# A two-layer diffusion transformer block on one core: z transposed whole behind the scores, squares moved behind the scores, partial sums stored by SyncE's queue

## The chip, the cores and the metric

The kernel runs on one core of one Trainium2 chip. The metric is the device time of one execution in microseconds (us), the median of three runs. A core has five engines that run at the same time, each through its own queue of instructions: PE (TensorE, with its weight loads listed apart as PEld), DVE (VectorE), ACT (ScalarE), POOL (GpSimd) and SP (SyncE, which only starts transfers). A transfer is issued from the queue of SP or ACT, waits there for what it needs, and holds up what stands behind it in that queue.

## The reference

Two layers work on 1024 latent tokens and 256 context tokens of width 1024, all in f32:

```python
p = h @ w_in                        # h: modulated RMS norm of x; hc likewise of the context
a_in, b_in, q, k, v, g = ...        # column ranges of p
q, k = rope(rms_norm(q)), rope(rms_norm(k))
s = q @ k.T * QK_DIM ** -0.5        # 4 heads, 2 maps each, keys of context and latents
p = softmax(s); p = p[0] - lam * p[1]
o = rms_norm(p @ v) * (1 - lam_init)
y = concat(fourier_mix(a_in), pool_mix(b_in), o) * silu(g)
x = x + gate * (y @ w_out)
```

The context tokens are updated in the first layer only, and attend to the context alone. Shift, scale and gate come from a conditioning vector times `w_mod`, for each layer.

## The kernel before, in words

Each f32 operand of a large product is split into two parts, high and low, and a product is three matmuls. The order on each engine is the order in which the code is written; nothing is rescheduled. Tiles come from rotating pools: `T5` and `E2` in SBUF, `PX` for banks of PSUM. `full` is true in layer 0, which also treats the ten tiles of latents and context (numbers 0 to 7 and 8, 9).

A layer has two phases. In the first (called phase A below) it builds the modulated rows H, mixes the Fourier and pooling heads, and computes half of the output projection, the part that needs no attention: `for hf in range(2): for j in range(nA)`, 12 matmuls (L751), DVE's product with the gate (L755), POOL's addition of the residual (L757), and a store of the partial sum to `xpart` (L759). `r_load` (L723) loads the residual two steps ahead through SP. Behind each step `next(bg)` runs one step of a background generator; in layer 0 that is `mod1`, the modulation of layer 1, whose weights are loaded through ACT's queue (L198) and summed by DVE (L207, L209, `total` with L237). Then follow the K, Q and V projections. K and Q use rotary tables that POOL makes (L773) from `gq`, `rcos` and `rsin`, loaded by SP (L764 to L767); L798 is the last step of a K or Q tile on DVE, and L786 its transposes on PE.

The second phase is attention, a loop of units (tile j, head h), four to a tile; in layer 0 there are two context units among them, at 4 and 13. That gives 34 units in layer 0 and 32 in layer 1. Step i runs parts of several units: transposes of the probabilities of unit i-2 (`p_trans`, L966, copied by ACT L971 and DVE L969), the scores of unit i (L899), row maxima (L908), exponentials (L923), products with V of unit i-2 (L982), the normalization by head (L985, L993, L1009), and pieces of the output projection of finished tiles (`out_proj`, L1048, added in L1051). The scores of a unit lie in two tiles of three PSUM banks each (one per map, `SS[0]` and `SS[1]`); `spare(cur, m)` hands out the last 256 columns of one of them before the scores are written. `q_trans` transposes the queries of the next tile into a `PX` bank behind the scores; `z_trans` transposes a finished tile's gated output z, in two halves, in the spare columns of `SS[1]` ahead of the scores. Both split the transposed rows with `trans_split`: PE transposes (L876), two copies by ACT (L877, L878) and a subtraction by POOL (L879). The four pieces of 256 columns follow at steps set by `PIECES`, `CTXP` and `LAST`. Tile 7, the last, is done in the tail.

In layer 0 a finished tile's rows are also squared and summed (`x_rms`, two halves, L265, driven by `tile_rms`) at the end of a step, and scaled by the result (L1065) for layer 1. Layer 0's tail is interleaved with the first rows of layer 1 (`h_block`; L279, L285; L1213 scales tiles that were reloaded). `wa_split`'s pieces split the output weights in early units (ACT L316, POOL L317).

Of the kernel before, what the change touches and what calls it, by code (L numbers as in the profile page):

```python
# [18 lines left out]
D = 1024  # L19
# [12 lines left out]
def build(tc, I, out):  # L32
# [156 lines left out]

    def mod_acc(src, c0, sides, res, eng2=None):  # L190

        acc = T5([128, 2, 512])
        res.append(acc)
        ws = []

        def load(kp):
            w = T5([128, 2, 512])
            act.dma_start(w, src[2 * kp:2 * kp + 2, :, c0:c0 + 512].rearrange("k p c -> p k c"))  # L198
            ws.append(w)
        load(0)  # L200
        load(1)
        yield
        for k in range(KT):
            for s in sides:
                a, w, sk = acc[:, s, :], ws[k // 2][:, k % 2, :], sc[:, k, s:s + 1]
                if k == 0:
                    dve.tensor_scalar(a, w, sk, None, MULT)  # L207
                else:
                    dve.scalar_tensor_tensor(a, w, sk, a, MULT, ADD)  # L209
            if k % 2 and k // 2 + 2 < KT // 2:  # L210
                load(k // 2 + 2)
            yield
# [15 lines left out]
    def mod1():  # L228
# [11 lines left out]
        for q in range(4):  # L240
            accs = []
            for n, _ in enumerate(mod_acc(I["wmB"], q * 512, (0, 1), accs)):
                if n == 4 and last is not None:
                    total(q - 1, last)
                yield
# [285 lines left out]
    def layer(l, src, dst, carry):  # L531
# [208 lines left out]
        for hf in range(2):  # L740
# [3 lines left out]
            for j in range(nA):  # L744
# [13 lines left out]
                r_load(hf * nA + j + 2)  # L758
                act.dma_start(xpart[l][j][:, sl], x)  # L759
                next(bg, None)  # L760
# [85 lines left out]
        k_trans(0)  # L846
        k_trans(0)
        st = {}

# [20 lines left out]

        def trans_split(rows, to, ps, h0, n):

            sl = slice(h0 * 128, h0 * 128 + n * 128)
            for h in range(n):
                o = (h0 + h) * 128
                pe.transpose(ps[:, h * 128:h * 128 + 128], rows[:, o:o + 128], ident)  # L876
            act.activation(to[0][:, sl], ps[:, :n * 128], AF.Copy)  # L877
            act.activation(rows[:, sl], ps[:, :n * 128], AF.Copy)  # L878
            pool.tensor_tensor(to[1][:, sl], rows[:, sl], to[0][:, sl].bitcast(F32), SUB)  # L879

        def q_trans(j):
            st[j]["Q"] = parts(j)
            trans_split(st[j]["q"], st[j]["Q"], PX(), 0, NH)

# [66 lines left out]

        def spare(cur, m):

            return st[cur]["SS"][m][:, 1280:1536] if cur else PX()

        def p_trans(u, t0, cur=None):
# [6 lines left out]
            n = min(4, nkt - t0)  # L963
            ps = spare(cur, 0) if t0 == 8 else PX()
            for i in range(n):
# [44 lines left out]

        def z_trans(j, half, cur):
            s = st[j]
            if half == 0:
                s["z"] = parts(j)
            trans_split(s["g"], s["z"], spare(cur, 1), 2 * half, 2)

# [13 lines left out]

        PIECES = [(c, 256, 2 + c // 256) for c in range(0, D, 256)]
        CTXP = [(c, 256, 3 + c // 256) for c in range(0, D, 256)]
        LAST = {7: [(0, 512, 2), (512, 512, 3)]} if full else {7: [(0, 512, 2), (512, 256, 3), (768, 256, 3)]}
        LAST.update({8: CTXP, 9: CTXP})
        ENDS = () if full else (6, 7)
# [38 lines left out]
        for i, u in enumerate(units):  # L1076
            first.setdefault(u[0], i)
        q_load(0)
        vv = []
# [15 lines left out]
        def step(i):  # L1095
# [3 lines left out]
            done = units[i - 3] if 0 <= i - 3 < N else None  # L1099

            fin = {d: units[i - 2 - d][0] for d in range(7)
                   if 0 <= i - 2 - d < N and units[i - 2 - d][1] in (NH - 1, -1)}
            if old and old[1] in (2, -1):
                out_load(old[0])
            if cur:
                st[cur] = dict(S=[], p=[], l=[], SS=[PS(), PS()])
            if old:
                p_trans(old, 0)
                p_trans(old, 8, cur)
            for d, half in ((1, 0), (2, 1)):  # L1110
                j = fin.get(d)
                if j is not None and j < 7:
                    z_trans(j, half, cur)
            for d, half in ((2, 0), (3, 1)):
                if fin.get(d, 0) >= 8:
                    z_trans(fin[d], half, cur)
            if old:
# [27 lines left out]
            yield  # L1145
            for d, j in sorted(fin.items(), key=lambda f: f[1]):
                for c0, m, at in LAST.get(j, PIECES):
                    if d == at:
                        out_proj(j, c0, m)
            if fin.get(1) == 7:  # L1150
                z_last(7)
            while rms:
                if next(rms[0], rms) is rms:
                    rms.pop(0)
                elif cur:
                    break
            if full:
                for d, j in fin.items():
                    if d == LAST.get(j, PIECES)[-1][2]:
                        rms.append(tile_rms(j))  # L1160
            yield
# [175 lines left out]
```

## Time and profile before

| | before |
|---|---|
| median of three runs | 1462.04 us (1458.29 to 1462.25) |
| the profiled execution | 1462.49 us, span 1460.7 us |
| granted TensorE clock, mean | 0.978 |
| PE, PEld busy | 1371.1 us (94%), 1223.1 us (84%) |
| DVE, ACT, POOL busy | 857.6 us (59%), 534.3 us (37%), 779.7 us (53%) |
| layer 0's attention, first and last scores start at | 522.1, 778.7 us |
| layer 1's attention, first and last scores start at | 1167.8, 1430.3 us |

The span is what the profiler shows of the execution's own time; 1.8 us lie around it. Busy shares are over the whole span. In the rows below, a timeline row gives start, duration, engine, line, operation, output and inputs, and in brackets the idle time before it and what ended it; a group's row gives count, busy time, mean of one in ns, and idle time before the group with what ended it. An engine name with q (ACTq, SPq) is its queue of transfers; a transfer's row there shows how long its issue held the queue, waits for its inputs included.

### The profile page before, as it was taken

The numbers are of one execution on the slowest core, as the hardware profiler recorded it, in microseconds if no ns is written. First come the engines' busy times: TensorE is split into PE (matmuls) and PEld (weight loads), VectorE is DVE, ScalarE is ACT, GpSimd is POOL, SyncE is SP. The second block draws the span as 40 slices with busy tenths as digits, with TensorE's granted clock in tenths as the row PEclk, the third lists the DMA queues.
The fourth block names the chain that finished last, engine by engine and source line by source line (L and its number), as shares of the span: only waits on it lengthen the run. The fifth ranks groups of instructions, "written<-read, shape, count | busy, mean of one in ns | idle before, by whom it ended". The sixth has DMA issues, their size and how long they took to land.

```text
span 1460.7 us, 24849 instructions
## 1 busy us (share of the span) xinstructions
PE 1371.1 (94%) x9828; PEld 1223.1 (84%) x9828; DVE 857.6 (59%) x1338; ACT 534.3 (37%) x1178; POOL 779.7 (53%) x867
## 2 busy tenths in 40 slices
PE   7899999897999978999998899999999998999998
PEld 1688899787999967978887778887999986788887
DVE  2853467787873056767665654573455225777775
ACT  2633111101221256565554432211131225665663
POOL 2543122457583057777775743226757217777774
PEclk9999999998999999999999999999999999999999
DMA  9320242584232022120213221526402210121111
GB/s 361 111 69 33 100 137 95 194 270 138 73 106 83 1 94 87 50 76 22 87 38 116 98 65 37 204 79 204 154 30 95 73 44 25 34 70 62 44 38 58
DMA packets 65155, 137.11 MB, mean 94 GB/s; under 512 B 7312, under 2 KB 19728, under 8 KB 65040
## 3 DMA queue, kind: packets, MB, share of 16 engines
q1 hardware_dynamic: 49712, 108.82, 22.3%
q10 hardware_dynamic: 15328, 26.72, 5.3%
q8 instruction: 77, 1.26, 0.4%
q14 instruction: 38, 0.31, 0.1%
HBM read 105.63 MB, written 29.88 MB: 93 GB/s over the span
## 4 chain that ended last, share of the span: by engine, by line
PE 36%; ACT 6%; DVE 5%; POOL 2%; issue 2%; DVEq 0%; ACTq 0%; POOLq 0%
PE x L359 13%; PE S L899 6%; PE x L339 5%; ACT t L923 4%; PE x L982 3%; PE x L751 3%; PE x L1048 2%; DVE sm L908 2%; PE x L966 1%; POOL t L288 1%; PE S L876 1%; POOL t L1052 0%; DVE e L285 0%; ACT t L286 0%; PE x L876 0%
## 5 line engine op out<-in xcount | busy, mean ns | idle before, releaser
L359 PE MATMUL x<-wh,t 128*128 128x256 f32 x2432 | 449.6, 285 | 0.0
L359 PEld LDWEIGHTS x<-wh,t 128*128 128x128 f32 x2432 | 383.0, 192 | 1.8 <-issue 1.0
L359 PE MATMUL x<-wl,t 128*128 128x256 f32 x1216 | 344.8, 284 | 0.0
L908 DVE TENSOR_REDUCE sm<-S 128x1 f32<-128x1280 f32 (+1 forms) x132 | 189.6, 1478 | 191.3 <-PE S L899 191.3
L359 PEld LDWEIGHTS x<-wl,t 128*128 128x128 f32 x1216 | 234.0, 192 | 1.3 <-issue 1.2
L923 ACT ACTIVATE t<-S,sm 128x1280 f32<-128x1280 f32 (+1 forms) x140 | 172.6, 1238 | 151.2 <-DVE sm L908 137.8
L339 PE MATMUL x<-t,wh 128*128 128x512 f32 (+1 forms) x640 | 174.2, 382 | 9.2 <-DVE t L288 4.6
L899 PE MATMUL S<-t,e 64*128 64x512 f32 (+1 forms) x1152 | 149.3, 381 | 24.2 <-ACT t L971 20.7
L982 PE MATMUL x<-t,t 128*128 128x128 f32 x1312 | 164.8, 282 | 6.3 <-DVE t L969 6.3
L982 PEld LDWEIGHTS x<-t,t 128*128 128x128 f32 x1312 | 154.2, 194 | 13.0 <-DVE t L969 6.5
L899 PEld LDWEIGHTS S<-t,e 64*128 64x128 f32 x1152 | 111.4, 193 | 61.8 <-ACT t L971 29.9
L339 PEld LDWEIGHTS x<-t,wh 128*128 128x128 f32 x640 | 114.5, 192 | 32.8 <-POOL t L288 6.2
L317 POOL TENSOR_TENSOR wl<-st,wh 128x1024 fp32r<-128x1024 f32 x36 | 93.9, 2609 | 87.3 <-ACT wh L316 87.3
L946 POOL TENSOR_TENSOR t<-t,t 128x768 f32<-128x768 f32 (+1 forms) x64 | 115.0, 1796 | 5.3
L316 ACT ACTIVATE wh<-st 128x1024 fp32r<-128x1024 f32 x64 | 65.0, 1063 | 135.6 <-DMA xpart<-e 53.3
L1048 PE MATMUL x<-wh,e 128*128 128x256 f32 (+1 forms) x488 | 105.5, 299 | 0.8 <-ACT e L1024 0.7
L339 PE MATMUL x<-t,wl 128*128 128x512 f32 (+1 forms) x320 | 100.6, 375 | 3.4 <-DVE wl L317 3.4
L751 PE MATMUL x<-wh,t 128*128 128x512 f32 x288 | 93.9, 405 | 7.8 <-DVE t L527 4.7
L209 DVE SCALAR_TENSOR_TENSOR t<-t,sc,t 128x512 f32<-128x512 f32 x98 | 90.7, 968 | 3.8 <-DMA t<-in_wmB_dram 3.4
L1048 PEld LDWEIGHTS x<-wh,e 128*128 128x128 f32 x488 | 80.7, 191 | 2.9 <-ACT e L1024 1.3
L997 POOL TENSOR_SCALAR sm<-sm,sm 128x1 f32<-128x1 f32 x64 | 16.9, 264 | 122.6 <-ACT t L993 116.6
L966 PE MATMUL x<-ident,t 128*128 128x128 f32 x520 | 79.6, 276 | 1.7 <-ACT t L971 0.9
(233 smaller groups left out, 2287.6 us busy)
## 6 DMA issues: line engine op xcount, KB each, us to landing
st<-in_w_in_dram SPq DMA_DIRECT2D x48, 512.0 KB, 4.5
t<-in_wmB_dram ACTq DMA_DIRECT2D x24, 512.0 KB, 5.3
xpart<-e ACTq DMA_DIRECT2D x36, 256.0 KB, 4.8
t<-xpart SPq DMA_DIRECT2D x18, 512.0 KB, 4.8
t<-in_wmS_dram SPq DMA_DIRECT2D x16, 512.0 KB, 8.5
st<-in_w_out_dram SPq DMA_DIRECT2D x16, 512.0 KB, 3.9
t<-in_x_dram SPq DMA_DIRECT2D x10, 512.0 KB, 10.3
e<-in_x_dram SPq DMA_DIRECT2D x20, 256.0 KB, 5.1
```

The costliest lines, as they stand in the source:

```text
L209: dve.scalar_tensor_tensor(a, w, sk, a, MULT, ADD)
L317: lo_eng[hf].tensor_tensor(lo[:, sl, :], st, hi[:, sl, :].bitcast(F32), SUB)
L339: pe.matmul(p[:, :m], lhsT=W[wi][:, k, ct * 128:ct * 128 + 128], rhs=H[k][hi][:, c0:c0 + m], start=(n == 0), stop=(n == 3 * KT - 1))
L359: pe.matmul(bank[:, i * 256:i * 256 + 256], lhsT=H[k][hi][:, j * 128:j * 128 + 128], rhs=W[wi][:, k, :], start=(n == 0), stop=(n == 3 * KT ...
L751: pe.matmul(ps, lhsT=zr[k][zi][:, j * 128:j * 128 + 128], rhs=W[wi][:, k, :], start=(n == 0), stop=(n == 11))
L899: pe.matmul(S[m][:, i * nk + c:i * nk + c + w], lhsT=Q[q][r, h * 128:h * 128 + 128], rhs=k[h][r, k0 + c:k0 + c + w], start=(n == 0), stop= ...
L908: dve.tensor_reduce(nb, S[:, :nh * nk].rearrange("p (h k) -> p h k", h=nh), AX.X, ALU.min)
L923: act.activation(p[:, sl], S[:, sl], AF.Exp, bias=nb[:, i:i + 1], scale=-1.0, accum_out=ls[:, i:i + 1])
L946: pool.tensor_tensor(p[0][:, cut:end], p[0][:, cut:end], p[1][:, cut:end], ADD)
L966: pe.transpose(ps[:, i * 128:i * 128 + 128], s["p"][0][:, (t0 + i) * 128:(t0 + i + 1) * 128], ident)
L982: pe.matmul(o[:, i * 128:i * 128 + 128], lhsT=s["PT"][:, i * nkt + t, :], rhs=vv[h][:, kt0 + t, :], start=(t == 0), stop=(t == nkt - 1))
L1048: pe.matmul(ps[:, :m], lhsT=s["z"][zi][:, k * 128:k * 128 + 128], rhs=Wa[hf][wi][:, k, w0:w0 + m], start=(n == 0), stop=(n == 11))
```

## The change

1. `z_trans` transposes all four heads at once into a `PX` bank, behind the scores and `q_trans`, by the same `trans_split` that `q_trans` uses. A small plan (`at_z`, `at_out`, `at_x`, `at_end`) replaces the tables: z of a tile comes at first + 8 (first + 5 for a context tile) or at the next step that no `q_trans` or other z has taken, the pieces in the four steps behind it, the load of the partial sum one step ahead of it. Before, the halves came at first + 6 and first + 7 (of tiles 0 to 6) and the pieces at first + 7 to first + 10.
2. The squares of `tile_rms` are issued behind the scores and transposes instead of at the step's end.
3. The stores to `xpart` go through SP's queue instead of ACT's.
4. `mod_acc` waits `lead` background steps between its first two loads and their first use (two in `mod1`), issues the third and fourth load at the start of steps 2 and 4 instead of at the end of steps 1 and 3, and what is left of the background generator runs behind the Q projection.

```diff
--- before.py
+++ after.py
@@ mod_acc @@
-    def mod_acc(src, c0, sides, res, eng2=None):
+    def mod_acc(src, c0, sides, res, lead=1):
...
-        yield
+        for _ in range(lead):
+            yield
         for k in range(KT):
+            if k in (2, 4):
+                load(k // 2 + 1)
...
-            if k % 2 and k // 2 + 2 < KT // 2:
-                load(k // 2 + 2)
             yield
@@ mod1 @@
-            for n, _ in enumerate(mod_acc(I["wmB"], q * 512, (0, 1), accs)):
+            for n, _ in enumerate(mod_acc(I["wmB"], q * 512, (0, 1), accs, 2)):
@@ half output projection @@
                 r_load(hf * nA + j + 2)
-                act.dma_start(xpart[l][j][:, sl], x)
+                sp.dma_start(xpart[l][j][:, sl], x)
                 next(bg, None)
@@ behind Q @@
         k_trans(0)
+        for _ in bg:
+            pass
@@ attention @@
-        def trans_split(rows, to, ps, h0, n):
...
+        def trans_split(rows, to):
+
+            ps = PX()
+            for h in range(NH):
+                pe.transpose(ps[:, h * 128:h * 128 + 128], rows[:, h * 128:h * 128 + 128], ident)
+            act.activation(to[0], ps, AF.Copy)
+            act.activation(rows, ps, AF.Copy)
+            pool.tensor_tensor(to[1], rows, to[0].bitcast(F32), SUB)
...
-            ps = spare(cur, 0) if t0 == 8 else PX()
+
+            ps = st[cur]["SS"][0][:, 1280:1536] if cur and t0 == 8 else PX()
...
-        def z_trans(j, half, cur):
-            s = st[j]
-            if half == 0:
-                s["z"] = parts(j)
-            trans_split(s["g"], s["z"], spare(cur, 1), 2 * half, 2)
+        def z_trans(j):
+            st[j]["z"] = parts(j)
+            trans_split(st[j]["g"], st[j]["z"])
...
-        PIECES = [(c, 256, 2 + c // 256) for c in range(0, D, 256)]
-        CTXP = [(c, 256, 3 + c // 256) for c in range(0, D, 256)]
-        LAST = {7: [(0, 512, 2), (512, 512, 3)]} if full else {7: [(0, 512, 2), (512, 256, 3), (768, 256, 3)]}
...
+        taken = {f - 1 for f in first.values()}
+        for j in sorted(first, key=first.get):
+            e = first[j] + (1 if j >= 8 else NH)
+            if j == 7:
+                plan(at_z, e + 2, j)
+                sizes = (512, 512) if full else (512, 256, 256)
+                steps_of = (e + 3, e + 4, e + 4)
+                plan(at_x, e + 1, j)
+            else:
+                z = e + 4
+                while z in taken:
+                    z += 1
+                taken.add(z)
+                plan(at_z, z, j)
+                sizes = (512, 512) if j == 6 else (256,) * 4
+                steps_of = range(z + 1, z + 5)
+                plan(at_x, z - 1, j)
...
-            for d, half in ((1, 0), (2, 1)):
-                j = fin.get(d)
-                if j is not None and j < 7:
-                    z_trans(j, half, cur)
...
+            for j in at_z.get(i, ()):
+                if j != 7:
+                    z_trans(j)
+            while rms:
+                if next(rms[0], rms) is rms:
+                    rms.pop(0)
+                elif cur:
+                    break
             if cur:
                 row_max(cur, 0)
                 row_max(cur, 1)
...
-            while rms:
-                if next(rms[0], rms) is rms:
-                    rms.pop(0)
-                elif cur:
-                    break
```

The order on PE ahead of the scores of a unit of layer 1, before (`x` is a PSUM bank, `S` a score tile, `ident` the identity of a transpose, `e_2066` the gated output of a finished tile, `t_2152` the probabilities):

```order
7235 L1048 MATMUL x_13703<-wh_12547,e_2082_13246 128x256
7236 L966 MATMUL x_13723<-ident,t_2152_13583 128x128 x4
7237 L966 MATMUL S_13720<-ident,t_2152_13583 128x128 x2
7238 L876 MATMUL S_13721<-ident,e_2066_13190 128x128 x2
7239 L966 MATMUL x_13737<-ident,t_2152_13583 128x128 x4
7240 L899 MATMUL S_13720<-t_1716_10620,e_2106_13382 128x512
7241 L899 MATMUL S_13721<-t_1716_10620,e_2106_13382 128x512
```

and ahead of the scores of the unit of layer 1 that holds the z of the tile in question now:

```order
7209 L1039 MATMUL x_13708<-wh_12488,e_2130_13384 128x256
7210 L965 MATMUL x_13727<-ident,t_2174_13583 128x128 x4
7211 L965 MATMUL S_13724<-ident,t_2174_13583 128x128 x2
7212 L965 MATMUL x_13736<-ident,t_2174_13583 128x128 x4
7213 L901 MATMUL S_13724<-t_1689_10235,e_2192_13670 128x512
7214 L901 MATMUL S_13725<-t_1689_10235,e_2192_13670 128x512
```

and behind its last scores (`e_2068` is the gated output):

```order
7229 L901 MATMUL S_13724<-t_1689_10235,e_2193_13671 128x256
7230 L901 MATMUL S_13725<-t_1689_10235,e_2193_13671 128x256
7231 L878 MATMUL x_13772<-ident,e_2068_13102 128x128 x4
7232 L981 MATMUL x_13788<-t_1811_11786,t_2208_13726 128x128 x10
7233 L1039 MATMUL x_13808<-wh_12488,e_2129_13383 128x256
```

The transposes of z into the score tile are gone from between those of the probabilities, and four of them stand behind the last scores, into a bank of their own.

ACT's queue in layer 0's half output projection before, stores and modulation loads in one line (`t_...<-in_wmB_dram` are the weights of `mod1`):

```order
175 L198 DMA t_401_2579<-in_wmB_dram 128x2x512
176 L198 DMA t_402_2581<-in_wmB_dram 128x2x512
177 L759 DMA xpart_104<-e_396_2554 128x512
178 L316 ACTIVATE wh_2604<-st_2379 128x1024
179 L316 ACTIVATE wh_2604<-st_2381 128x1024
180 L759 DMA xpart_104<-e_399_2575 128x512
181 L198 DMA t_413_2635<-in_wmB_dram 128x2x512
182 L759 DMA xpart_104<-e_405_2599 128x512
183 L759 DMA xpart_104<-e_412_2630 128x512
184 L198 DMA t_420_2679<-in_wmB_dram 128x2x512
185 L759 DMA xpart_104<-e_416_2653 128x512
```

SP's queue at the end of that projection now (`e_...<-in_x_dram` are residual loads, and the last three the tables' inputs):

```order
112 L760 DMA xpart_104<-e_418_2668 128x512
113 L724 DMA e_430_2745<-in_x_dram 128x512
114 L760 DMA xpart_104<-e_421_2689 128x512
115 L724 DMA e_434_2768<-in_x_dram 128x512
116 L760 DMA xpart_104<-e_427_2724 128x512
117 L724 DMA e_437_2789<-in_x_dram 128x512
118 L760 DMA xpart_104<-e_430_2745 128x512
119 L760 DMA xpart_104<-e_434_2768 128x512
120 L760 DMA xpart_104<-e_437_2789 128x512
121 L765 DMA gq_2835<-in_qkg_dram 128x256
122 L767 DMA e_446_2837<-in_rcos_dram 128x512
123 L768 DMA e_447_2838<-in_rsin_dram 128x512
```

The stores stand between the residual loads, and ahead of `gq`, `rcos` and `rsin`; ACT's queue keeps the modulation loads.

DVE in layer 0's tail before (L1065 scales a tile of layer 0 by its norm, L1213 the reloaded tiles, L969 copies transposed probabilities):

```order
663 L1051 TENSOR_TENSOR e_1351_8262<-x_8249,t_624_4925 128x256
664 L1065 TENSOR_SCALAR t_1164_7407<-t_1164_7407,r_109 128x1024
665 L1213 TENSOR_SCALAR t_1343_8224<-t_1343_8224,r_109 128x1024
666 L1213 TENSOR_SCALAR t_1344_8226<-t_1344_8226,r_109 128x1024
667 L1213 TENSOR_SCALAR t_1345_8228<-t_1345_8228,r_109 128x1024
668 L1213 TENSOR_SCALAR t_1346_8230<-t_1346_8230,r_109 128x1024
669 L969 COPY t_1353_8275<-x_8276 128x512
670 L1009 SCALAR_TENSOR_TENSOR e_1282_7952<-t_1304_8052,sm_8246,e_1282_7952 128x128
```

and now:

```order
661 L1042 TENSOR_TENSOR e_1353_8206<-x_8193,t_624_4925 128x256
662 L1221 TENSOR_SCALAR t_1345_8168<-t_1345_8168,r_109 128x1024
663 L1221 TENSOR_SCALAR t_1346_8170<-t_1346_8170,r_109 128x1024
664 L1221 TENSOR_SCALAR t_1347_8172<-t_1347_8172,r_109 128x1024
665 L1221 TENSOR_SCALAR t_1348_8174<-t_1348_8174,r_109 128x1024
666 L968 COPY t_1355_8216<-x_8217 128x512
667 L1056 TENSOR_SCALAR t_1227_7640<-t_1227_7640,r_109 128x1024
668 L1008 SCALAR_TENSOR_TENSOR e_1284_7897<-t_1305_7994,sm_8190,e_1284_7897 128x128
669 L1042 TENSOR_TENSOR e_1366_8273<-x_8260,t_624_4925 128x512
```

Tile 5's scaling by its norm (`t_1164` before, `t_1227` now) stood ahead of the four scalings and the copy, and now stands behind them.

More of the change, by code (lines that the diff above doesn't have):

```diff
@@ L869, in parts @@
             return [E2([128, 512], F32R) for _ in range(2)]
-        def trans_split(rows, to, ps, h0, n):
[L873 to L879, printed above, removed]
+        def trans_split(rows, to):
[5 more added lines that the diff above has]
+            pool.tensor_tensor(to[1], rows, to[0].bitcast(F32), SUB)
         def q_trans(j):
             st[j]["Q"] = parts(j)
-            trans_split(st[j]["q"], st[j]["Q"], PX(), 0, NH)
+            trans_split(st[j]["q"], st[j]["Q"])
         def rng(u):
@@ L950, in combine @@
             s["le"] = le
-        def spare(cur, m):
-            return st[cur]["SS"][m][:, 1280:1536] if cur else PX()
         def p_trans(u, t0, cur=None):
@@ L1029, in out_load @@
             sp.dma_start(st[j]["x"], xpart[l][j])
-        PIECES = [(c, 256, 2 + c // 256) for c in range(0, D, 256)]
-        CTXP = [(c, 256, 3 + c // 256) for c in range(0, D, 256)]
-        LAST = {7: [(0, 512, 2), (512, 512, 3)]} if full else {7: [(0, 512, 2), (512, 256, 3), (768, 256, 3)]}
-        LAST.update({8: CTXP, 9: CTXP})
         ENDS = () if full else (6, 7)
@@ L1077, in layer, with plan @@
             first.setdefault(u[0], i)
+        at_z, at_out, at_x, at_end = [{} for _ in range(4)]
+        def plan(d, i, v):
+            d.setdefault(i, []).append(v)
+        taken = {f - 1 for f in first.values()}
[15 more added lines that the diff above has]
+                plan(at_x, z - 1, j)
+            c = 0
+            for m, i in zip(sizes, steps_of):
+                plan(at_out, i, (j, c, m))
+                c += m
+            plan(at_end, steps_of[len(sizes) - 1], j)
         q_load(0)
@@ L1099, in step @@
             done = units[i - 3] if 0 <= i - 3 < N else None
[L1101 to L1104, printed above, removed]
+            for j in at_x.get(i, ()):
+                out_load(j)
             if cur:
@@ L1109, in step @@
                 p_trans(old, 8, cur)
-            for d, half in ((1, 0), (2, 1)):
-                j = fin.get(d)
-                if j is not None and j < 7:
-                    z_trans(j, half, cur)
-            for d, half in ((2, 0), (3, 1)):
-                if fin.get(d, 0) >= 8:
-                    z_trans(fin[d], half, cur)
             if old:
@@ L1145, in step @@
             yield
[L1146 to L1150, printed above, removed]
-                z_last(7)
-            while rms:
-                if next(rms[0], rms) is rms:
-                    rms.pop(0)
-                elif cur:
-                    break
+            for a in at_out.get(i, ()):
+                out_proj(*a)
+            if 7 in at_z.get(i, ()):
+                z_last(7)
             if full:
-                for d, j in fin.items():
-                    if d == LAST.get(j, PIECES)[-1][2]:
-                        rms.append(tile_rms(j))
+                for j in at_end.get(i, ()):
+                    rms.append(tile_rms(j))
             yield
```

## The prediction

> **What bounds the kernel now.** I read the page's table of engines first, then its groups by cost and by the wait ahead of them, then busy time in chosen stretches, then timelines of the few places that the change touches.
>
> ```profile
> PE 1371.1 (94%) x9828; PEld 1223.1 (84%) x9828; DVE 857.6 (59%) x1338; ACT 534.3 (37%) x1178; POOL 779.7 (53%) x867
> L899 PE MATMUL S<-t,e 64*128 64x512 f32 (+1 forms) x1152 | 149.3, 381 | 24.2 <-ACT t L971 20.7
> L316 ACT ACTIVATE wh<-st 128x1024 fp32r<-128x1024 f32 x64 | 65.0, 1063 | 135.6 <-DMA xpart<-e 53.3
> 573.64:778.71 205.07, 197.21 (x1631) 175.17 (x1631) 145.46 (x211) 125.90 (x316) 154.14 (x227) 1.00 0.17 56
> 1264.34:1430.33 165.99, 164.45 (x1364) 146.00 (x1365) 119.68 (x176) 100.07 (x232) 120.04 (x172) 1.00 0.14 47
> ```
>
> TensorE (PE) is the bound, so the change can give no more than PE's waits and the stretching of its work. The score matmuls (L899) own the largest wait, 24.2 us, nearly all for ScalarE's copy of transposed probabilities (L971). The two stretches (length, then busy us of PE, PEld, DVE, ACT, POOL, then clock) are the attention loops of layer 0 and layer 1. ScalarE's wait of 53.3 us for a partial sum's buffer (L316's row) is the store queue, of which more below. Layer 1's loop looks full, 164.45 of 165.99 us, but a matmul that stands between waiting neighbours is counted busy. The timeline of one latent tile there (four units) shows it:
>
> ```profile
> 1294.47 2.01 PE L899 MATMUL S<-t,e 64*128 64x512 f32 x18 [0.16 <-ACT t L971]
> 1301.12 0.44 PE L876 MATMUL S<-ident,e 128*128 128x128 f32 x2
> 1301.92 2.40 PE L899 MATMUL S<-t,e 64*128 64x512 f32 x18
> 1309.66 2.40 PE L899 MATMUL S<-t,e 64*128 64x512 f32 x18
> 1311.99 0.66 PE L876 MATMUL x<-ident,e 128*128 128x128 f32 x4
> 1317.44 2.01 PE L899 MATMUL S<-t,e 64*128 64x512 f32 x18
> 1324.65 1.66 PE L899 MATMUL S<-t,e 64*128 64x512 f32 x12 [0.16 <-ACT t L971]
> ...
> 1301.59 0.38 ACT L877 ACTIVATE e<-S 128x256 fp32r<-128x256 f32 x1
> 1301.87 0.38 ACT L878 ACTIVATE e<-S 128x256 f32<-128x256 f32 x1
> 1321.14 1.33 ACT L923 ACTIVATE t<-S,sm 128x1280 f32<-128x1280 f32 x1 [3.02 <-DVE sm L908]
> ```
>
> Score starts are 7.45, 7.74, 7.78 and 7.21 us apart: 30.18 us in all. The two units with a half z (L876 into S) ahead of the scores take 2.40 us for scores that take 2.01 elsewhere, because the scores reuse the bank that L877 and L878 still read. The last unit has neither z nor q work: its chain (scores, row max, exponentials, copy, next scores) makes 7.2 us.
>
> **The change part by part.**
>
> *z whole behind the scores.* Four plain units would be 4 × 7.2 = 28.8; the 1.34 over that is two score stretches of 0.39, z halves ahead of scores (0.25 behind the first unit, 0.14 behind the second) and the q transposes (7.78 − 0.39 − 7.2 = 0.19 in the third). The change removes the z parts and adds four transposes behind the scores, 0.66 us like the q row (L876 into x), of which, as with q, 0.19 shows, because ScalarE's two copies lie in its 3.02-us gap ahead of the exponential. The period becomes 28.8 + 2 × 0.19 = 29.2, 0.97 less. If the stretches aren't recovered it is 0.2 less. The stretch of the loop shown holds 165.99 / 30.18 = 5.5 periods: −5.3 us, bounds −1 and −6.5 (if the new z shows nowhere). POOL's subtraction of the two parts has a whole unit before the first piece asks for it, and the load of the tile's partial sum on SP is issued a step ahead of z, two ahead of its use: 14 us, where a landing takes 5.1 (a row below); I cost both at nothing, and without that cover each tile would wait for a landing less what is left of it.
>
> *Squares behind the scores*, layer 0 alone. The rows:
>
> ```profile
> 606.20 0.63 ACT L265 ACTIVATE e<-t 128x512 f32<-128x512 f32 x1
> 606.72 0.20 ACT L265 ACTIVATION_READ_ACCUMULATOR e<-t 128x1 f32 x1
> ...
> 573.64 0.50 PE L899 MATMUL S<-t,e 64*128 64x512 f32 x1 [0.63 <-ACT t L971]
> 590.54 0.73 PE L899 MATMUL S<-t,e 64*128 64x512 f32 x4
> 599.08 0.50 PE L899 MATMUL S<-t,e 64*128 64x512 f32 x1
> 700.71 0.50 PE L899 MATMUL S<-t,e 64*128 64x512 f32 x2 [0.77 <-ACT t L971]
> 708.53 0.50 PE L899 MATMUL S<-t,e 64*128 64x512 f32 x1 [0.30 <-ACT t L971]
> 778.71 1.12 PE L899 MATMUL S<-t,e 64*128 64x512 f32 x5
> ```
>
> A square holds ScalarE 0.61 us right ahead of the copy that PE's scores wait for: a unit with one and nothing else takes 708.53 − 700.71 = 7.82, against layer 1's 7.2. Units with pieces of two tiles take longer: 599.08 − 590.54 = 8.54. From 573.64 to 778.71 are 25 units. After the change, by the planned steps, I count 8 plain units at 7.2, 5 with one q or z at 7.45, 5 with a z and a square at 7.9 (ScalarE's gap then holds the copy, 0.6, two z copies that start only when the scores and transposes end, and the square, so I leave the square's cost in), 3 with two pieces at 8.55, and 4 with two pieces and a z or q at 9.2 (8.55 + 0.66): 57.6 + 37.3 + 39.5 + 25.7 + 36.8 = 196.9, against 205.07. −8.2 us; bounds −5.5 (stretches kept) and −10.5 (squares free).
>
> *The early units* of each attention phase still split the output weights on ScalarE and POOL:
>
> ```profile
> 1225.04:1228.45 3.41, 1.44 (x6) 1.17 (x8) 1.14 (x3) 2.41 (x7) 2.52 (x3) 0.72 0.02 5
> 1227.01 3.34 PE L899 MATMUL S<-t,e 64*128 64x512 f32 x18 [2.04 <-ACT t L971]
> ```
>
> There the wait is ScalarE's queue and the granted clock falls to 0.72. The first tile's pieces now start two units later, which takes work from the same units but leaves PE emptier. I take −1.5 (±1.5) in layer 0, where two z halves and a context tile leave units 5 to 7, and 0 (±1.5) in layer 1.
>
> *Stores on SP's queue, loads earlier.* In layer 0's output projection the modulation loads (L198) stand on ScalarE's queue behind stores (L759) that wait for POOL:
>
> ```profile
> 320.86 12.39 ACTq L759 DMA_DIRECT2D xpart<-e  x5
> 333.35 0.95 ACTq L198 DMA_DIRECT2D t<-in_wmB_dram  x2
> ...
> 338.13 0.88 DVE L207 TENSOR_SCALAR t<-t,sc 128x512 f32<-128x512 f32 x2 [6.00 <-DMA t<-in_wmB_dram]
> 339.69 1.73 POOL L757 TENSOR_TENSOR e<-e,e 128x512 f32<-128x512 f32 x1 [5.55 <-DVE e L755]
> 341.38 6.45 POOL L773 TENSOR_TENSOR e<-e,gq 128x512 f32<-128x512 f32 x4
> 345.77 0.28 PE L359 MATMUL x<-wh,t 128*128 128x256 f32 x1
> 354.13 0.69 DVE L798 TENSOR_TENSOR e<-e,sm 128x512 f32<-128x512 f32 x1 [0.92 <-POOL e L827]
> 354.87 1.11 PE L786 MATMUL x<-ident,e 128*128 128x128 f32 x4 [8.83 <-DVE e L798]
> ...
> 334.25 0.33 SPq L767 DMA_DIRECT2D e<-in_rsin_dram  x1
> e<-in_x_dram SPq DMA_DIRECT2D x20, 256.0 KB, 5.1
> ```
>
> The chain reads forward: late loads stop DVE 6.00 us, POOL's last add waits, so do the rotary tables (L773), and their end puts the first K tile at PE 8.83 us late. With the loads issued a step earlier, on a queue that no longer holds stores, DVE no longer waits; its last product (L755) then falls near 330 instead of 339, and POOL's add of 1.73 follows. What is late next is the tables' inputs: gq, rcos, rsin are queued on SP behind the last store, which waits for that add. One landing of 3 to 5 us (the row of 5.1) behind 330 puts L773 near 334. From L773 to PE's transposes are 354.87 − 341.38 = 13.5, so PE would start at 347.5 and wait 1.5 instead of 8.83: −7.5. If the tables start at 338 it is −4; if nothing waits and the slow clock behind the stall goes too, −10.5. On SP each residual load (L723) is now behind a store that waits for POOL's add of the step before; it is asked for two steps ahead, 8 us or so, against 5.1 us of landing, so I cost it at nothing; without that cover each of 20 steps would pay up to its landing. The background work now has more steps than the loops call, so its last sums run at once behind Q: the same instructions, taken as nothing, with at worst one 1 us wait inside the bounds. Layer 1 has no modulation loads, and I take nothing there.
>
> *The tails.* A z at first+8 and pieces behind it push two 256-column pieces behind the last scores, each 1.44 us (the first row, from the chain of waits; the others from timelines):
>
> ```profile
> 1427.42 1.44 PE x L1048 x12
> 797.97 4.64 PE L982 MATMUL x<-t,t 128*128 128x128 f32 x20 [6.30 <-DVE t L969]
> 794.58 2.74 DVE L1213 TENSOR_SCALAR t<-t,r 128x1024 f32<-128x1024 f32 x4
> 815.74 2.83 DVE L1065 TENSOR_SCALAR t<-t,r 128x1024 f32<-128x1024 f32 x1 [3.07 <-POOL r L268]
> 819.77 0.50 PE L339 MATMUL x<-t,wl 128*128 128x512 f32 x1 [3.38 <-DVE wl L317]
> ```
>
> Layer 1's tail is all PE, so it grows by 2 × 1.44 + 0.3 = +3.2. Layer 0's tail gets the same work, but PE stands 6.30 there for a DVE copy (L969) behind four scalings of layer 1's rows (L1213) and one tile's norm (L1065), and 3.38 for a weight split (L317) behind another norm; in the new order the first norm follows the copy, and the last but one is earlier. Half of each, 4.8, less 3.2 gives −1.6; bounds −4 and +3.
>
> The sum: −7.5 − 1.5 − 8.2 − 1.6 + 0 − 5.3 + 3.2 = −20.9 us. The profiled execution took 1462.49 (a span of 1460.7 and 1.8 around it), 0.45 above the median shown; so 1441.6, and I say 1442.
>
> **The rivals.**
>
> *Half of it.* The stall moves instead of going: stores, residual loads and tables share one queue, so the tables start at 339 and phase A gives −3; score stretches turn into waits for ScalarE and the loops give −5.5 and −1; early units and the tail of layer 0 give 0. With +3.2 that is −6.3, or 1456. For it: layer 1's loop is 99% busy. Against: the 2.40 beside the 2.01 can hardly be anything but the shared bank.
>
> *It doesn't do what it says.* SP's order keeps the whole 8.83, the layer 0 tail takes its +3, the loops give −4 and −1: +1.2 with layer 1's tail, 1464. For it stands that the tables' own loads were late before (rsin issued at 334.25); against it, that they then waited for buffers whose stores stood on the slow queue.
>
> *Slower, by the clock.* With z two steps later PE has less to do ahead of each first piece, and a unit whose PE idles 2.04 us ran its scores at 3.34 instead of 2.01. Each unit that falls into this loses 1.33 us; from 16 such units the gain of 20.9 is gone, from 19 the kernel is slower by over 4.4; 22 would give 1471. The Trainium skill (TensorE: Matmul & The Clock Gate, HAM oscillation) states the rule as no PE-idle gaps over about 3.4 us; by it gaps of 2 us would cost no clock here and this rival would fall to nothing. The trace doesn't agree: 0.72 was granted with no gap over 2.04. Against the rival stands that both loops' rows have 1.00, and layer 0's with 7.9 us of idle in 205.
>
> **How the numbers follow.** A measurement of this kernel can tell about 0.3%, 4.4 us, from no change. Forecast as worked out, 1430 to 1451: 0.62. Half: 0.18. No change: 0.12. Slower: 0.08. All terms at their gainful ends give −32.8, so the low end is 1430; the high end, 1457, takes in the half case and leaves out the last two, 0.20 together. Faster is 0.62 + 0.18 = 0.80.
>
> **What would show it.** Right: scores at 2.0 us in every steady unit and a layer 1 period near 29.2; no modulation wait on DVE ahead of the K projection, and PE's wait there under 3 us; layer 0's 25 units in about 197; some 3 us more behind layer 1's last scores. Wrong: a wait of the old size for rcos or rsin on POOL, a clock under 1 in the steady loops, squares that delay the exponential, or a layer 0 tail that waits for its rows.

## The result and the profile after

The changed kernel takes 1443.49 us (median of four, 1436.60 to 1446.82) against 1461.85 us for the kernel before (four runs now): a ratio of 0.9874, with a 95% interval of 0.9831 to 0.9917. The forecast was 1442. A second set of four, beside the experiments, gave 1442.08 and a ratio of 0.9874 (0.9839 to 0.9908). The profiled execution took 1440.90 us, with a span of 1439.1.

The table of engines, the score group, and the two attention loops of the changed kernel, layer 0's from the scores of its unit 8 and layer 1's from those of its unit 9 to those of the last unit, as in the rows of before (lines are one or two up on those of before, L901 for L899 and so on):

```profile
PE 1352.0 (94%) x9780; PEld 1210.2 (84%) x9780; DVE 860.0 (60%) x1332; ACT 537.7 (37%) x1146; POOL 787.2 (55%) x849
L901 PE MATMUL S<-t,e 64*128 64x512 f32 (+1 forms) x1152 | 135.3, 377 | 27.9 <-ACT t L970 26.9
563.24:758.36 195.12, 189.79 (x1620) 171.28 (x1620) 146.12 (x208) 127.75 (x301) 155.19 (x218) 0.99 0.21 73
1245.04:1405.48 160.44, 158.49 (x1361) 142.75 (x1362) 121.56 (x176) 99.82 (x219) 120.45 (x164) 1.00 0.15 49
```

PE's share is still 94%, so the shares alone tell nothing. The score matmuls are busy 135.3 us instead of 149.3, while the wait ahead of them has grown a little: what went is the stretching. The timeline of one tile of layer 1 shows it:

```profile
1288.68 2.01 PE L901 MATMUL S<-t,e 64*128 64x512 f32 x18 [0.16 <-ACT t L970]
1290.62 0.66 PE L878 MATMUL x<-ident,e 128*128 128x128 f32 x4
1296.06 2.01 PE L901 MATMUL S<-t,e 64*128 64x512 f32 x18
1298.00 0.65 PE L878 MATMUL x<-ident,e 128*128 128x128 f32 x4
1303.45 2.01 PE L901 MATMUL S<-t,e 64*128 64x512 f32 x18
1310.65 1.67 PE L901 MATMUL S<-t,e 64*128 64x512 f32 x12 [0.16 <-ACT t L970]
```

No score of the steady units (9 and later, in both layers) takes 2.40 us any more; q and z are the two rows of L878. The unit starts are 7.38, 7.39 and 7.20 us apart, the next scores start at 1317.88, and the period of four is 29.2 us where it was 30.18. The 0.99 in layer 0's row is a low granted clock in unit 8; from 567 us on it is 1.00.

Distances between fixed points of the traces (the first matmul of layer 0's half output projection behind its 4.1 us wait, score starts by unit, the end) put the terms side by side:

| stretch | predicted | before, us | changed, us | changed again, us |
|---|---|---|---|---|
| start to half projection | 0 | 264.79 | 261.31 | 262.94 |
| from there to layer 0's unit 2 | -7.5 | 257.31 | 253.61 | 251.49 |
| layer 0, units 2 to 8 | -1.5 | 51.54 | 48.32 | 52.38 |
| layer 0, units 8 to 33 | -8.2 | 205.07 | 195.12 | 193.59 |
| unit 33 to layer 1's unit 2 | -1.6 | 425.87 | 428.47 | 428.31 |
| layer 1, units 2 to 9 | 0 | 59.76 | 58.21 | 56.59 |
| layer 1, units 9 to 31 | -5.3 | 165.99 | 160.44 | 160.30 |
| layer 1's tail | +3.2 | 30.37 | 33.62 | 33.60 |

The first line is not the change's doing. Up to 90 us both kernels run the same code; the granted clock differs, as the same 20 us of before and of the changed kernel show:

```profile
60.00:80.00 20.00, 16.58 (x84) 15.04 (x83) 16.14 (x40) 6.01 (x13) 2.08 (x2) 0.74 0.30 86
```

```profile
60.00:80.00 20.00, 16.87 (x105) 14.89 (x104) 17.68 (x43) 7.04 (x14) 4.38 (x5) 0.91 0.30 86
```

Nearly all of the 3.5 us arises there: one and the same matmul starts at 67.03 us before and 66.68 now, another at 89.63 and 86.14, and from this one to the half projection it is 175.16 and 175.17 us. In between runs `gate_rows`, which uses `mod_acc` too, so that its third and fourth loads also come a step later; that moved nothing.

In the first phase of layer 0 PE still waits, 6.38 us instead of 8.83 (5.04 in the changed kernel's second profile), now for the tables' inputs. Rows of SP's queue, POOL and PE in the changed kernel:

```profile
328.54 0.33 SPq L767 DMA_DIRECT2D e<-in_rcos_dram  x1
...
334.90 5.05 POOL L774 TENSOR_TENSOR e<-e,gq 128x512 f32<-128x512 f32 x4 [7.53 <-DMA e<-in_rcos_dram]
...
346.29 1.11 PE L787 MATMUL x<-ident,e 128*128 128x128 f32 x4 [6.38 <-DVE e L799]
```

In layer 0's tail the wait of 6.30 has shrunk to 3.81, but DVE stands for stores of rows that it is about to overwrite (`x<-t`), and PE waits for the weight split behind it and for the last tile's norm:

```profile
770.86 3.87 DVE L1221 TENSOR_SCALAR t<-t,r 128x1024 f32<-128x1024 f32 x4
777.97 0.75 DVE L1056 TENSOR_SCALAR t<-t,r 128x1024 f32<-128x1024 f32 x1 [2.65 <-DMA x<-t]
792.72 0.75 DVE L1056 TENSOR_SCALAR t<-t,r 128x1024 f32<-128x1024 f32 x1 [4.68 <-DMA x<-t]
...
775.38 4.02 PE L981 MATMUL x<-t,t 128*128 128x128 f32 x20 [3.81 <-DVE t L968]
796.58 0.73 PE L340 MATMUL x<-t,wh 128*128 128x512 f32 x2 [1.86 <-ACT wh L317]
798.59 0.50 PE L340 MATMUL x<-t,wl 128*128 128x512 f32 x1 [1.27 <-DVE wl L318]
812.05 0.33 PE L280 MATMUL x<-ident,t 128*128 128x128 f32 x1 [2.20 <-DVE t L1056]
```

### The profile page after: what moved, and what is told of

It reads as the page before. It is cut to its first block, busy times and chain, and to the rows that moved or that the text cites. A ratio compares the mean times of both kernels' runs of the same rounds, so it can differ in the third digit from the quotient of the medians.

```text
span 1439.1 us, 24628 instructions
## 1 busy us (share of the span) xinstructions
PE 1352.0 (94%) x9780; PEld 1210.2 (84%) x9780; DVE 860.0 (60%) x1332; ACT 537.7 (37%) x1146; POOL 787.2 (55%) x849
## 4 chain that ended last, share of the span: by engine, by line
PE 57%; ACT 10%; DVE 7%; issue 3%; POOL 3%; DMA 2%; SPq 0%; DVEq 0%; ACTq 0%; POOLq 0%
PE x L360 22%; PE S L901 10%; ACT t L925 6%; PE x L752 6%; PE x L981 5%; PE x L340 5%; PE x L1039 4%; DVE sm L910 3%; PE x L965 2%; PE x L878 1%; ACT t L970 1%; ACT t L992 1%; DMA e<-in_x_dram 1%; ACT wh L317 1%; POOL t L289 1%
## 5 line engine op out<-in xcount | busy, mean ns | idle before, releaser
L360 PEld LDWEIGHTS x<-wh,t 128*128 128x128 f32 x2432 | 382.6, 192 | 1.8 <-issue 1.0
L340 PE MATMUL x<-t,wh 128*128 128x512 f32 (+1 forms) x640 | 173.6, 381 | 10.5 <-DVE t L289 4.3
L981 PE MATMUL x<-t,t 128*128 128x128 f32 x1312 | 162.8, 280 | 4.1 <-DVE t L968 3.8
L901 PE MATMUL S<-t,e 64*128 64x512 f32 (+1 forms) x1152 | 135.3, 377 | 27.9 <-ACT t L970 26.9
L981 PEld LDWEIGHTS x<-t,t 128*128 128x128 f32 x1312 | 153.7, 194 | 9.0 <-DVE t L968 4.0
L901 PEld LDWEIGHTS S<-t,e 64*128 64x128 f32 x1152 | 103.5, 193 | 60.0 <-ACT t L970 39.8
L318 POOL TENSOR_TENSOR wl<-st,wh 128x1024 fp32r<-128x1024 f32 x36 | 93.1, 2585 | 80.5 <-ACT wh L317 80.5
L1039 PE MATMUL x<-wh,e 128*128 128x256 f32 (+1 forms) x456 | 102.4, 306 | 0.9 <-ACT e L1021 0.7
L212 DVE SCALAR_TENSOR_TENSOR t<-t,sc,t 128x512 f32<-128x512 f32 x98 | 86.1, 921 | 4.1 <-DMA t<-in_wmB_dram 3.7
L1039 PEld LDWEIGHTS x<-wh,e 128*128 128x128 f32 x456 | 75.8, 190 | 4.1 <-DVE e L1022 1.1
L752 PEld LDWEIGHTS x<-wh,t 128*128 128x128 f32 x288 | 55.8, 195 | 20.6 <-DVE t L528 5.6
```

The lines of the kernel that those rows point to most:

```text
L318: lo_eng[hf].tensor_tensor(lo[:, sl, :], st, hi[:, sl, :].bitcast(F32), SUB)
L340: pe.matmul(p[:, :m], lhsT=W[wi][:, k, ct * 128:ct * 128 + 128], rhs=H[k][hi][:, c0:c0 + m], start=(n == 0), stop=(n == 3 * KT - 1))
L360: pe.matmul(bank[:, i * 256:i * 256 + 256], lhsT=H[k][hi][:, j * 128:j * 128 + 128], rhs=W[wi][:, k, :], start=(n == 0), stop=(n == 3 * KT ...
L752: pe.matmul(ps, lhsT=zr[k][zi][:, j * 128:j * 128 + 128], rhs=W[wi][:, k, :], start=(n == 0), stop=(n == 11))
L901: pe.matmul(S[m][:, i * nk + c:i * nk + c + w], lhsT=Q[q][r, h * 128:h * 128 + 128], rhs=k[h][r, k0 + c:k0 + c + w], start=(n == 0), stop= ...
L981: pe.matmul(o[:, i * 128:i * 128 + 128], lhsT=s["PT"][:, i * nkt + t, :], rhs=vv[h][:, kt0 + t, :], start=(t == 0), stop=(t == nkt - 1))
```

## The experiments

### Each edit alone

Four kernels take one edit each on the kernel before. Z alone: the new plan and `z_trans(j)`, without the other three edits.

> The kernel before with the z transposes whole behind the scores and the new plan of pieces, nothing else. Theory (the scores stood behind the z copies): layer 1's units 8 to 31 take 167.7 us as in the changed kernel (173.7 before), its tail 33.6 (30.4 before); layer 0's units 8 to 33 about 199 to 201 (205.1 before, 195.1 changed), since the squares stay in front of the copies; phase A keeps its 8.8 us wait. In all -9 to -14 us. Rival (the score stretch only turns into another wait): layer 1's units stay above 172 and the kernel is within 4 us of the one before.

Measured: 1456.46 us, ratio 0.9974 (0.9953 to 0.9995): 3.6 us faster and not 9 to 14, by the time alone the rival's number. The stretches tell more. Layer 1's units 9 to 31 take 160.31 us, as in the changed kernel, so the theory holds there; its tail takes 33.7. Layer 0's units 8 to 33 take 202.06, less gain than expected. Against before these three are -5.7, +3.3 and -3.0, and layer 0's tail stretch is +2.8: -2.6 together. The reason for layer 0's small gain is in this timeline (PE, then ACT):

```profile
725.04 2.01 PE L898 MATMUL S<-t,e 64*128 64x512 f32 x18
732.85 2.01 PE L898 MATMUL S<-t,e 64*128 64x512 f32 x18 [0.76 <-ACT t L967]
740.66 1.19 PE L898 MATMUL S<-t,e 64*128 64x512 f32 x8 [0.76 <-ACT t L967]
...
731.80 0.63 ACT L265 ACTIVATE e<-t 128x512 f32<-128x512 f32 x1
```

The scores are at 2.01, yet the units are 7.81 long: a square stands ahead of the copy that they wait for.

The squares alone:

```diff
+            while rms: ...     # behind score, q_trans and z_trans
             if cur:
                 row_max(cur, 0)
...
-            while rms: ...     # at the end of the step
```

> The kernel before with only the squares moved behind the scores. Theory (each square delays the copy ahead of the scores by 0.6 us, where no z half does it anyway): layer 0's units 8 to 33 fall from 205.1 to about 200 to 202, nothing changes elsewhere, -3 to -5 us. Rival (the squares now delay the exponential, or PE is the bound of those units): within 2 us of before in those units.

Measured: 1458.23 us, 0.9988 (0.9961 to 1.0016). Layer 0's units 8 to 33 take 200.63, inside the expectation; the whole is 1.9 us faster, not 3 to 5, and the timed runs can't tell it from no change. Here the other half of the pair is left:

```profile
726.52 2.01 PE L899 MATMUL S<-t,e 64*128 64x512 f32 x18 [0.17 <-ACT t L971]
733.17 0.44 PE L876 MATMUL S<-ident,e 128*128 128x128 f32 x2
733.97 2.39 PE L899 MATMUL S<-t,e 64*128 64x512 f32 x18
```

The queue alone is the one line `sp.dma_start(xpart[l][j][:, sl], x)`.

> The kernel before with only the stores of partial sums on SP's queue. Theory (the modulation loads stood behind the stores on ScalarE's queue): VectorE's 6.0 us wait for a load ahead of the K projection goes, the tables start some 6 us sooner, PE's wait there is 6 to 7 instead of 8.8, and from the first matmul of the half output projection to the scores of unit 2 it is 253 to 255 us (257.3 before, 253.6 changed). Rival (the later issue of loads in the background work is the cause): 256 us or more and VectorE's wait stays above 3 us.

Measured: 1460.31 us, 1.0002 (0.9979 to 1.0025); from the half projection to unit 2 it is 254.02, 3.3 less than before and as expected, and DVE's 6.0 us wait is gone; the timed runs don't show the 3.3. PE's wait is 8.12, not 6 to 7, since PE too arrives earlier. POOL and PE in it:

```profile
336.46 5.02 POOL L773 TENSOR_TENSOR e<-e,gq 128x512 f32<-128x512 f32 x4 [6.74 <-DMA e<-in_rcos_dram]
...
348.52 1.11 PE L786 MATMUL x<-ident,e 128*128 128x128 f32 x4 [8.12 <-DVE e L798]
```

The lead alone, with stores on ScalarE's queue:

```diff
-        yield
+        for _ in range(lead):
+            yield
         for k in range(KT):
+            if k in (2, 4):
+                load(k // 2 + 1)
```

> The kernel before with only the changed lead and load steps of the background work and its rest behind the Q projection; stores stay on ScalarE's queue. Theory (queue): loads still stand behind stores, so a wait of several us on VectorE remains, and the same distance is 256 to 259 us. Rival (lead): 253 to 255 us, as in the changed kernel.

Measured: 1463.09 us, 1.0009 (0.9988 to 1.0031); the distance is 257.26. The loads still stand behind stores, as rows of DVE and ACT's queue show:

```profile
290.58 1.42 DVE L212 SCALAR_TENSOR_TENSOR t<-t,sc,t 128x512 f32<-128x512 f32 x2 [4.85 <-DMA t<-in_wmB_dram]
...
329.74 9.41 ACTq L760 DMA_DIRECT2D xpart<-e  x4
339.24 0.96 ACTq L198 DMA_DIRECT2D t<-in_wmB_dram  x2
```

None of the four reaches a third of the whole gain: the medians move by -3.6, -1.9, +0.2 and +3.0 us, -2.3 together, where the change gives -18; only z's interval leaves out no change at all.

### In pairs

Z and squares, with stores and background loads as before:

> Both attention edits (whole z, squares behind the scores), with the stores on ScalarE's queue and the background loads as before. Theory (each of the two leaves the other's wait standing ahead of the scores, so together they give more than their sum): layer 0's units 9 to 33 take 186 to 187 us, as in the changed kernel (197.1 before, 193.4 with z alone, 192.6 with the squares alone); the kernel is 9 to 13 us faster than before. Rival (the changed kernel's gain needs the queue edits): layer 0's units at 189 us or more, or the whole less than 7 us faster.

Measured: 1447.82 us, 0.9910 (0.9882 to 0.9939), 12.8 us faster. Layer 0's units 9 to 33 take 186.46 us, as in the changed kernel (186.48). Its timeline at the place shown above:

```profile
721.40 2.00 PE L898 MATMUL S<-t,e 64*128 64x512 f32 x18
728.60 2.01 PE L898 MATMUL S<-t,e 64*128 64x512 f32 x18 [0.16 <-ACT t L967]
735.81 2.01 PE L898 MATMUL S<-t,e 64*128 64x512 f32 x18 [0.16 <-ACT t L967]
```

Plain units of 7.2 us in a row come only with both: units 27 and 28 of layer 0 take 7.20 and 7.21 us here, 7.81 each with z alone, 7.45 and 7.72 with the squares alone. In units 9 to 33 the parts give 3.6 and 4.5 us alone and 10.6 together, so 2.5 is their interaction. The medians give 5.5 for the two alone, added, and 12.8 together. Of these 7.3 more, what lies over the 2.5 is not in the steady units; with intervals of 3 to 4 us either way on each of the three runs it can be noise.

Queue and lead:

> Both edits of the first phase (stores on SP's queue, loads and lead of the background work), attention as before. Theory: from the first matmul of the half output projection to the scores of unit 2 about 253.6 us (257.3 before, 254.0 with the queue alone), so the pair is worth 2 to 4 us and the lead almost none of it. Rival (the two need each other): 6 us or more.

Measured: 1455.19 us, 0.9967 (0.9944 to 0.9990), 5.4 us faster; the distance is 251.93, a gain of 5.4, between the expectation and its rival. PE's wait is 5.26. One profile of each puts the lead's share at about 2 us over the queue alone. The five profiles with both edits (this one, the changed kernel's two, e9 and e10 below) spread from 249.2 to 253.6, all under the queue's 254.02. By the medians the pair gives 5.6 more than the queue alone; the traces don't place what is over the 2.

The changed kernel again:

> The changed kernel once more, beside the others on the same chip. If the parts explain it, it is the pair of attention edits plus the pair of queue edits: 13 to 18 us faster than before, 1441 to 1447. If its first four runs were lucky, less than 12 us.

Measured: 1442.08 us, 18.5 us faster, just over the 13 to 18 expected; the two pairs' 12.8 and 5.4 add to 18.2.

### What the queue edit left

The tables' inputs earlier:

```diff
             for j in range(nA):
+                if hf == 1 and j == nA - 4:
+                    gq, rt = ...        # the same three loads on SP
...
-        sp.dma_start(rt[0], I["rcos"])  # with gq and rsin, behind the loop
```

> The changed kernel with the loads of gq, rcos and rsin issued in the second half of the output projection loop, four steps before its end, instead of behind the last store. Theory (the 6.4 us that PE still waits ahead of the first K tile are the landing of these loads): the tables start right behind POOL's last sum, 6 to 7 us sooner, PE's wait falls under 1 us, and the kernel is 5 to 7 us faster than the changed one. Rival (the next thing late is a weight split or DVE's own queue): the wait falls to 3 us or more and the gain is under 4 us.

Measured: 1435.80 us, 0.9825 (0.9786 to 0.9864), 6.3 below the changed kernel beside it. Rows of SP's queue, POOL and PE:

```profile
321.46 0.40 SPq L750 DMA_DIRECT2D e<-in_rcos_dram  x1
...
332.95 5.06 POOL L773 TENSOR_TENSOR e<-e,gq 128x512 f32<-128x512 f32 x4
...
344.42 0.66 PE L786 MATMUL x<-ident,e 128*128 128x128 f32 x4 [1.53 <-DVE e L798]
```

The tables start at POOL's last sum without a wait, and PE waits 1.53 us, a little over the 1 expected. The distance from the half projection to unit 2 is 245.30, against 251.49 of the changed kernel in the same set and 249.2 in the lowest profile of that code. The landing was the wait.

### What ate the tail

Two changes to layer 0's tail, on the changed kernel. First:

```diff
-                dve.tensor_scalar(x, x, r1[:, j:j + 1], None, MULT)
+                if j in (5, 6): pend.append((x, j))   # scaled at the end of the step
+                else: dve.tensor_scalar(x, x, r1[:, j:j + 1], None, MULT)
```

> The changed kernel; in layer 0's tail the scalings of tiles 5 and 6 by their norms, which overwrite rows that a store is still reading, stand one step's length later on VectorE. Theory (what ate the tail's gain is VectorE standing 2.7 and 4.7 us for these stores, behind which layer 1's rows and a weight split wait): both waits go, PE's waits of 1.9 and 1.3 us for the weight split go, and from the scores of unit 33 of layer 0 to those of unit 2 of layer 1 it is about 425.5 us (428.4 in the changed kernel, 425.9 before). Rival (the tail is longer by its two moved pieces alone): 428 us or more.

Measured: 1442.95 us, 0.9871 (0.9840 to 0.9901), no difference from 1442.08 that the runs can tell; the distance is 426.33, near the 425.5 expected. DVE's wait of 2.7 us for a store is gone, and of the 4.7 a wait of 1.58 is left. PE's waits for the weight split fell from 3.1 to 0.8, but part of it came back at the last tile's norm, for which PE waits 3.82 instead of 2.20:

```profile
772.86 3.92 PE L981 MATMUL x<-t,t 128*128 128x128 f32 x20 [3.80 <-DVE t L968]
793.76 0.51 PE L340 MATMUL x<-t,wl 128*128 128x512 f32 x1 [0.80 <-DVE wl L318]
807.25 0.33 PE L280 MATMUL x<-ident,t 128*128 128x128 f32 x1 [3.82 <-DVE t L1059]
```

The chain of waits from 785 to 808 us names who sets that: POOL, with layer 1's rows (L289), sums of pieces (L1043) and a weight split (L318).

```profile
by line: POOL t L289 35.2%; POOL t L1043 20.6%; DVE t L1059 12.3%; POOL wl L318 10.3%; POOL r L269 9.1%; issue 7.4%; ACT e L266 3.2%; PE x L340 2.5%; POOL r L268 1.7%; POOL r L267 1.6%; PE x L280 1.4%; POOLq L318 0.2%
```

Second, the four scalings of reloaded tiles go from the end of step N to behind the first part of step N+1:

> As e9_scale_later, and the four scalings of reloaded tiles stand behind the copy of transposed probabilities that PE waits 3.8 us for, not ahead of it. Theory: this wait falls under 1 us and the same distance is about 422.5 us, 6 less than in the changed kernel. Rival (the scalings now delay the rows or products behind them): 425 us or more.

Measured: 1439.36 us, 0.9857 (0.9836 to 0.9878); the distance is 422.58, 5.9 less than the changed kernel's 428.47, and the 3.81 is gone altogether (the row of L981 has no wait):

```profile
773.90 2.50 PE L981 MATMUL x<-t,t 128*128 128x128 f32 x20
```

The wait for the last norm stays, at 3.80. The medians, 1439.36 here and 1442.08 in another set, couldn't tell the gain from nothing; it is read from the trace.

### Together

> e8_tables_loaded_early and e10_scale_later_and_behind together, on the changed kernel. If both act at their own places, the sum of their gains, 11 to 13 us less than the changed kernel: 1429 to 1432. If one only moves a wait, no better than e8_tables_loaded_early, 1435 or more.

Measured: 1430.48 us (1429.51 to 1431.17), ratio 0.9793 (0.9779 to 0.9808): 30 us below the kernel before beside it and some 12 below the changed one's 1442.08, of another set. The trace has both gains: 246.16 us from the half projection to unit 2, and 423.38 in the tail's stretch. The two add.

The plan moved by one step (`taken = {f - 2 ...}`, `z = e + 3`, `q_trans` at first - 2, `q_load` at first - 4):

> As e11_better, with each z one step earlier (first + 7) and each q transposes and load one step earlier too, so that no unit has both. Theory (a piece moved out of the tail costs its 1.44 us of PE only where PE is full, and units 7 and 8 have idle PE): layer 1's tail is about 1.7 us shorter (33.6 in the changed kernel), layer 0's as much, the loops stay as they are: 2 to 4 us better than e11_better. Rival (buffers of the earlier q make the loop wait, or the early units slow by the clock): no better, or slower.

Measured: 1433.15 us, 0.9814 (0.9796 to 0.9832), no better. Layer 0's units 9 to 33 take 188.46 us instead of 186.45: they hold one piece more (372 matmuls of `out_proj` instead of 360), 1.44 us of PE, and PE is idle 0.7 us longer in them. Layer 0's tail stretch is shorter by 1.2 us only (422.14 for 423.38). Layer 1's tail is 33.76 us against 33.87 of e11_better, though it has a 256-column piece less. Two rows of it:

```profile
1410.27 0.41 PE L964 MATMUL x<-ident,t 128*128 128x128 f32 x2 [0.44 <-DVE e L1041]
1418.64 0.33 PE L1018 MATMUL x<-ident,e 128*128 128x128 f32 x1 [1.44 <-DVE e L1007]
```

The last of the transposes of tile 7's z (L1018) now waits 1.44 us for DVE's normalization by head (L1007). In e11_better two 512-column pieces of tile 6 stand on PE between the last products with V and these transposes, which wait for nothing; here one of the two was done a step earlier. The wait is as long as the 256-column piece that left the tail.

## Why the prediction was right, point by point

**Z behind the scores.** The mechanism was right and the size too: period 29.2 as predicted, 5.6 us in layer 1's units 9 to 31 for 5.3, and e1_z_only gives that by itself. The rival that stretches turn into ScalarE's waits is refuted by it.

**Squares.** Right in kind; the sum for layer 0's loop, -8.2, was short of -10.0 and -11.5, the second beyond its bound of -10.5. The two differ in unit 8, which took 8.64 us at a low clock and 7.16 at a full one; units 9 to 33 alone give -10.6 in both. The step that failed is the 7.9 for units with a z and a square: those five take 7.4 to 7.7 us. Units with two pieces and a z or q took 8.5 to 8.9, not 9.2. That the two edits need each other the prediction had implicitly, by costing final units, and did not say.

**The stall.** The term was mis-sized: -7.5 predicted, -3.7 and -5.8 measured, the first just outside its lower bound of -4. The step that failed is "One landing of 3 to 5 us (the row of 5.1) behind 330". Times counted from the first matmul of the half output projection leave out the clock ahead of it. So counted, the tables were to start at 69.2 us (334 less 264.79) and started at 73.6 and 72.3. The text counts the landing from DVE's last product; but POOL's last sum ended at 66.1, the load of `rcos` behind it was issued at 67.2, and the tables started 6.4 and 5.1 us after that. That 334.90 stands near the 334 of the text is luck: 3.5 us of it are the clock ahead of the phase. PE was ready for the transposes at 78.6 and 78.7 instead of 81.3, which the text left out, and so waited 6.38 and 5.04 us, not 1.5. e8_tables_loaded_early shows that the landing is the cause.

**Layer 0's tail.** The wrong sign: +2.6 and +2.4 for -1.6, inside the stated bounds of -4 and +3. The step that failed is "Half of each, 4.8": PE's waits of 6.30 and 3.38, 9.7 us, became waits of 3.81, 1.86, 1.27 and 2.20, 9.1 us, and the two pieces came on top. Two causes are shown. DVE's scalings stood for stores that still read the rows: with two of them later the stretch is 2.1 us shorter (e9). The four scalings of reloaded tiles still stood ahead of the copy: with them behind it, it is 3.7 us shorter again (e10), 5.9 in all. The prediction looked at DVE's order and not at what the scaling overwrites.

**Layer 1's tail** is +3.25 for +3.2: right.

**The early units** gave more than the -1.5 and 0 predicted. Over all profiles, units 2 to 9 of layer 0 take 61.2 us on the mean in the five kernels with half z's and 58.5 in the nine with whole ones; in layer 1 60.0 and 58.0. One kernel differs from profile to profile by as much, so the means say that it didn't get worse, and the size of the gain is open. Between the scores of units 0 and 12 half the clock was granted for 11.6 us on the mean with half z's and 12.1 with whole ones in layer 0, and for 10.9 and 9.9 in layer 1: the rival by the clock is refuted. Where the rest of the interaction of z and squares lies, if it is more than noise, stays open.

**The signs.** Of the text's signs of being wrong, three showed: `rcos` kept POOL waiting (7.53 us), the clock of layer 0's loop read 0.99 (unit 8 alone), and layer 0's tail waited for its rows. Of its signs of being right one did not come, a wait of PE under 3 us ahead of the K projection.

The total fell within 2 us of the forecast partly by luck, because misses cancelled: the stall and the first tail gave 6 to 8 us less, layer 0's loop, layer 1's early units and, in the profiles, the clock of the first 265 us made up for it.

## What to carry to other kernels

A unit's length tells more than an engine's share: PE was 94% busy before and after, and a part of the gain sat in scores at 2.40 us that take 2.01 alone. Where two things stand one beside the other ahead of the same wait, each edit alone shows little; try them in pairs before dropping either. A load moved behind other work on a queue is priced from issue to landing at the place where it is used, and an in-place update is priced with the store that still reads the rows.

## What the runs showed of the hardware

The clock in the early units depends on when they fall. The same kernel in two profiles (score starts and lengths of layer 1's units 5 to 7, the changed kernel first, then again):

```profile
1209.28 3.30 PE L901 MATMUL S<-t,e 64*128 64x512 f32 x18 [2.04 <-ACT t L970]
1218.72 3.41 PE L901 MATMUL S<-t,e 64*128 64x512 f32 x18 [2.05 <-ACT t L970]
1228.27 2.83 PE L901 MATMUL S<-t,e 64*128 64x512 f32 x18 [2.05 <-ACT t L970]
```

```profile
1211.18 2.01 PE L901 MATMUL S<-t,e 64*128 64x512 f32 x18 [2.05 <-ACT t L970]
1219.33 2.37 PE L901 MATMUL S<-t,e 64*128 64x512 f32 x18 [2.00 <-ACT t L970]
1228.51 2.01 PE L901 MATMUL S<-t,e 64*128 64x512 f32 x18 [2.09 <-ACT t L970]
```

With idle times of 2.0 to 2.1 us in both, the scores take 3.3, 3.4 and 2.8 us in the one and 2.0, 2.4 and 2.0 in the other. Windows of 3.41 us around unit 6, in the same order (behind the length, PE's busy time; third from the end, the granted clock):

```profile
1215.52:1218.93 3.41, 1.06 (x8) 0.85 (x10) 2.04 (x6) 3.41 (x10) 1.29 (x3) 1.00 0.02 5
1218.93:1222.34 3.41, 3.41 (x19) 2.62 (x18) 0.11 (x1) 0.23 (x1) 3.33 (x3) 0.50 0.08 10
```

```profile
1217.36:1220.77 3.41, 1.44 (x12) 1.22 (x14) 1.14 (x3) 2.40 (x7) 2.52 (x3) 1.00 0.02 5
1220.77:1224.18 3.41, 3.41 (x20) 3.11 (x19) 2.38 (x2) 0.79 (x1) 3.33 (x3) 0.50 0.38 84
```

In each of the 14 profiles the granted clock is 1.00 or 0.50 and changes only on a grid of 3.41 us, and the grid lies elsewhere against the kernel in each of these two. Of the windows on that grid that had the full clock, all 156 in which PE was busy under 1.5 us are followed by one at half, 22 of the 67 with 1.5 to 1.9 us, and 5 of the 5387 with more. So an idle time counts by what it leaves of one window: the same 2 us cost clock where they fall into one, and not where two windows share them. The Trainium skill (TensorE: Matmul & The Clock Gate, Part 1: The HAM clock gate) says that the window in which activity is counted runs freely and does not start with the kernel; the rows agree. The rule of the Trainium skill (the same page, HAM oscillation) that there be no PE-idle gaps over about 3.4 us is not enough by these rows: gaps of 2 us cost clock here.
